# Loading the first quarter's mixed rows during the attention, and transposing the last samples' output behind three output tiles

## The chip, the cores and the metric

The kernel runs on one core of a Trainium2 chip. The core has five engines that run their own instruction queues and wait for each other on semaphores: TensorE (PE), VectorE (DVE), ScalarE (ACT), GpSimd (POOL) and SyncE (SP, which here only issues transfers). Sixteen DMA engines move data between the memory of the chip and the on-chip buffers; a transfer is issued from the queue of SP, ACT or POOL. The metric is the time of one execution on the device in microseconds (us); lower is better.

## The reference: what is computed

One layer of a decoder, for a prompt of 1024 tokens and for 8 samples of 8 new tokens each (together 1088 token columns), all in float32:

```python
h = rms_norm(x, norm1) * (1 + scale1) + shift1
z = h @ w_in                      # split into q, keys, values, gates, conv and pool inputs
o_attn = g[0] * o_cmp + g[1] * o_slc + g[2] * o_win     # three attention branches, gated
y_conv = conv_bg * short_conv(conv_cg * conv_h)
y_pool = multi_pool(pool_in)
x = x + gate1 * (concat[o_attn, y_conv, y_pool] @ w_out)
h = rms_norm(x, norm2) * (1 + scale2) + shift2
x = x + gate2 * (silu(h @ w_up_a) * (h @ w_up_b)) @ w_down
```

The compressed branch of the attention works on blocks of the keys and values that a small network (`compress`) makes; for the samples these come from a paged cache of 4096 positions each. The concatenation that goes into `w_out` is called the mixed rows here: 1024 channels (8 groups of 128) by 1088 columns.

## The kernel before

**Stages.** `build` runs three stages after one another. The first is the input projection, with the convolution and the pooling. The second is the attention: the prompt's (`prompt_attention`, 32 units of one block of 128 queries, one half of the heads and one branch, counted by `v_done`), the samples' (`sample_attention`, four pairs of samples with nine pieces each, counted by `u_done`) and beside them the compression of the samples' caches (`compress`, one batch per sample, counted by `cmp_done`). The third, `tail`, is the output projection, the norm, the up projection (in products of half matrices) and the down projection. A large product is made of three products of rounded parts: an operand is split by ACT into a high part (`split`, L175) and by DVE or POOL into the rest (L171), and `mm3` multiplies high by high, high by low and low by high.

**The mixed rows.** All three mixers write their part of the mixed rows to the buffer `mix_d` in the chip's memory: the convolution and the pooling in the first stage, the prompt's attention at L1205 after each second unit, and the samples' attention in `sample_combine` (L1406 on). The latter, once for each pair of samples `p`, makes on DVE a weighted sum of twelve partial results (`co`, L1428), transposes it on PE (`tr`, L143), copies it by DVE into `smo` (L1435) and stores it from SP's queue (L1439) into the columns from 1024 + 16 p.

**The output projection.** `output_projection` treats the 1088 columns as four quarters of 272. It goes through three groups: quarter 0, quarter 1, and quarters 2 and 3 together. In each group there are 8 output tiles `m` of 128 channels; a tile takes 24 matmuls of 272 columns for each quarter. `load` fetches a weight tile (`w_raw`, L1489, three buffers, SP's queue), `split` cuts it into `w_hi` and `w_lo` (two halves, nine buffers each). `fetch` (L1514) brings two channel groups of the mixed rows into `mixc` (four buffers), from SP's queue for quarter 0 and from ACT's for the others, and `mix` splits them into `mh` and `ml`. `x_load` (L1540) brings the rows of x from ACT's queue. The result of a tile goes by DVE (L1468) into x and from there to memory (`x_d`, L1559).

**What sets the order.** The program is a set of tasks (generators) with priorities; `run` picks the next one by an account of time that `use` keeps for each engine, and `yield` gives the account's time at which a task can go on. The framework below it then puts every engine's instructions in an order by its own simulated timeline. An engine works its queue strictly in that order. A buffer that is used again waits until what it held has been read. The pools of buffers lie on two stacks (left, right); a pool that is opened later takes the place of a closed one and waits for what lay there.

**What the change touches.** The buffers of `compress` and `compress_post` are `vt`, `pre`, `ksq`, `vcT` and `kvo` (L549 to L656), one of each. Their result is stored from POOL's queue (`cmp_d`, L669). The up projection keeps its hidden rows in `f_g` (L1662, four buffers).

Of the kernel before, what the change touches and what calls it, by code (L numbers as in the profile page):

```python
# [7 lines left out]
F32 = mybir.dt.float32  # L8
# [9 lines left out]
P = 128  # L18
D = 1024
KT = D // P  # L20
SEQ = 1024
NB = 8
NT = 8
# [3 lines left out]
HALF = 272  # L27
# [35 lines left out]
class Kernel:  # L63
# [476 lines left out]
    def compress(self, pool, batches, ahead):  # L540
        nc = self.nc
        last = batches[-1] * 4 + 3 + ahead
# [3 lines left out]
        for b in batches:  # L546
            yield from self.hold(lambda: self.post_free)
            self.post_free = False
            vt = pool.tile([P, 2, 256], F32, name="vt")  # L549
            pre = pool.tile([P, 2, 256], F32, name="pre")  # L550
            nc.vector.memset(pre[:, :, 255:256], 0.0)
            for half in range(2):
                uv = (yield from self.bank_of("S")).rearrange("p (v n) -> p v n", v=2)
                for q in range(2):
                    i = b * 4 + half * 2 + q
                    self.compress_load(i)
                    t, at = self.raw[i]
# [11 lines left out]
                r = self.compress_evac(uv, vt, pre, half)  # L569
# [22 lines left out]
    def compress_prompt(self, pool):  # L592
# [14 lines left out]
        self.post_free = False  # L607
        vt = pool.tile([P, 2, 256], F32, name="vt")
        pre = pool.tile([P, 2, 256], F32, name="pre")
        uv = (yield from self.bank_of("S")).rearrange("p (v n) -> p v n", v=2)  # L610
# [7 lines left out]
    def compress_post(self, pool, b, vt, pre, r, w=256):  # L618
# [16 lines left out]
        self.post_free = True  # L635
        sq = pool.tile([P, 256], F32, name="ksq")[:, 0:w]
        nc.scalar.activation(sq, o[0][:, 0:w], AF.Square)
        vc = pool.tile([P, 256], F32, name="vcT")[:, 0:w]
        nc.vector.tensor_copy(vc, o[1][:, 0:w])
# [9 lines left out]
        if b is None:  # L649
            self.tr(m[0:w, 256:256 + P], vc)  # L650
            nc.vector.tensor_copy(self.vcp, m[0:w, 256:256 + P])
            key, f = self.kcp, lambda a: a
        else:
            for h in range(2):
                self.tr(m[:, 256 + h * P:256 + (h + 1) * P], vc[:, h * P:(h + 1) * P])
            kv = pool.tile([P, 2, 256], F32, name="kvo")  # L656
            nc.vector.tensor_copy(kv[:, :, P:2 * P], m[:, 256:512].rearrange("p (h d) -> p h d", h=2))
            key, f = kv[:, :, 0:P], lambda a: a.rearrange("p (h c) -> p h c", h=2)
# [747 lines left out]
    def sample_combine(self, pool, st, p):  # L1406
# [16 lines left out]
        for x, (a, b) in enumerate(br):  # L1423
            nc.vector.tensor_scalar(w[:, a:b], w[:, a:b], ds_[:, 2 + x:3 + x], None, op0=OP.mult)
        o = pool.tile([P, P], F32, name="co", bufs=2)
        nc.vector.tensor_scalar(o, part[:, 11], gr[:, 0:1], None, op0=OP.mult)
        for c in range(11):
            nc.vector.scalar_tensor_tensor(o, part[:, c], w[:, c:c + 1], o, op0=OP.mult, op1=OP.add)  # L1428
        yield self.use("dve", 4.0, self.t["pe"]) + 0.5
        tr = yield from self.bank_of("S")  # L1430
        self.tr(tr[:, 0:P], o)
        mo = pool.tile([P, 4, 2, NT], F32, name="smo", bufs=2)
        for g in range(2):
# [3 lines left out]
                tr[s, 0:P].rearrange("p (b g r t) -> p g b r t", b=2, g=2, r=4)[:, g])  # L1437
        self.give("S", self.use("dve", 0.4, self.t["pe"]))
        nc.sync.dma_start(self.mix_d[:, 0:4, SEQ + 16 * p:SEQ + 16 * p + 16],  # L1439
                            mo.rearrange("p r b t -> p r (b t)"))  # L1440
        self.combined = p + 1

# [13 lines left out]
    def sample(self, opened, cp, batches):  # L1456
        share = lambda: 1.9 + 0.4 * (self.cmp_done - EARLY) / (NB - EARLY)
        self.spawn(share, self.compress(cp, batches, 0))
        sp = opened.enter_context(self.pool("samp", "left"))
        yield self.t["dve"]  # L1460
        self.spawn(lambda: 2 + 1.1 * self.u_done / 36, self.sample_attention(sp))


    def residual(self, out, acc, m, c0, n, gate, x, pool):
# [4 lines left out]
        if np_ < n:  # L1469
# [3 lines left out]
            nc.vector.tensor_tensor(r(out), r(x), tmp, op=OP.add)  # L1473
        return self.use("dve", 0.13 + np_ * 0.00104 + (0.27 if np_ < n else 0), self.t["pe"] + 0.1)

    def halves(self, a):
# [15 lines left out]
    def output_projection(self, wp, pool, nt, x1, opened):  # L1492
# [3 lines left out]
        todo = [m for _ in groups for m in range(KT)]  # L1496
        raw, ws, mx, parts = [], [], [], {}

# [8 lines left out]

        order = [(c, k) for c in range(4) for k in range(0, KT, 2)]

        def fetch():  # L1510
            if order:
                c, k = order.pop(0)
                t = pool.tile([P, 2, HALF], F32, name="mixc", bufs=4)
                (nc.sync if c == 0 else nc.scalar).dma_start(t, self.mix_d[:, k:k + 2, c * HALF:c * HALF + HALF])  # L1514
                mx.append((c, k, t, self.use("dma", 0.8, self.t["pe"]) + 2.2))
# [10 lines left out]

        fetch()
        load()
        for _ in range(3):
            fetch()  # L1530
        load()
# [12 lines left out]
        for cs in groups:  # L1544
            ss = {c: nt.tile([P, HALF], F32, name="n_ss", bufs=2) for c in cs}
            for m in range(KT):
                w = ws.pop(0)
                load()
                for c in cs:
                    yield max(w[0][2], parts[c, 0][2])  # L1550
                    acc = self.bank()
                    for k in range(KT):
                        wk = [self.halves(a)[:, k % 4] for a in w[k // 4][:2]]
                        self.mm3(acc[:, :HALF], wk, parts[c, k][:2], k == 0, k == KT - 1)
                    if c == cs[-1]:
# [103 lines left out]
    def up(self, fp, j, p, W, H, step):  # L1659
        nc = self.nc  # L1660
        bank = {}
        g = fp.tile([P, 2, HALF], F32, name="f_g", bufs=4)  # L1662
        t1 = lambda name: fp.tile([P, HALF], F32, name=name, bufs=1)
# [463 lines left out]
    def build(self):  # L2127
# [16 lines left out]
        self.tok_last = None  # L2144
        self.constants()
        st_ = self.pool("stream", "left")
        self.stream = st_.__enter__()
# [169 lines left out]
```

## Time and profile before

| | |
|---|---|
| median of 3 runs | 1677.42 us (1677.28 to 1678.26) |
| the profiled execution's own time | 1670.79 us |
| its span, first to last instruction | 1669.2 us |
| PE busy in the span | 1565.7 us, 94% |
| DVE, ACT, POOL busy | 1092.0, 777.8 and 660.9 us |
| mean granted TensorE clock | 0.975 |
| end of the attention's last matmul | 818.67 us |
| first matmul of the output projection | 834.46 us |

Times in the views are microseconds from the start of the span. A line of the timeline has the start, the duration, the engine, the line of the kernel with the operation, what is written and read, how many instructions are merged, and in brackets the idle time of the engine before it with what ended it. "SPq" and "ACTq" are the transfers that these queues issue. In a view of the waits a line says who waited for whom, in total us, how often, and the longest.

### The profile page before, as it was taken

The page shows a single profiled execution, that of the slowest core. Times are in us where ns is not written, and L with a number is a line of the kernel's source. Part 1 is how long each engine was busy: PE and PEld are TensorE (multiplying, and loading weights), DVE is VectorE, ACT ScalarE, POOL GpSimd, SP SyncE. Part 2 cuts the span into 40 slices and gives each one's busy share as a digit, 9 for nine tenths or more (in the row PEclk, how much of TensorE's full clock was granted, in tenths as well). Part 3 has the DMA queues.
Part 4 walks back from the last instruction along what each step waited for, and adds up shares of the span by engine and source line. Part 5 has one row for each costly group of instructions (what it writes and reads, how often), then busy time and mean ns, then how long its engine had stood idle before and what let it go on. Part 6 is the DMA issues. An engine that isn't in the chain of part 4 may idle for free. (4 is left out here: it accounts for less than half of the span.)

```text
span 1669.2 us, 35421 instructions
## 1 busy us (share of the span) xinstructions
PE 1565.7 (94%) x12569; PEld 1390.4 (83%) x12569; DVE 1092.0 (65%) x2633; ACT 777.8 (47%) x1829; POOL 660.9 (40%) x789
## 2 busy tenths in 40 slices
PE   6998999997999899899599989999999999899998
PEld 2898897896777666566399989999999999899988
DVE  4713233887555566766589878777777775577695
ACT  3522114335766667666467534433334433344463
POOL 3120110114333223223003366554555554778695
PEclk9999999998999899999899999999999999999999
DMA  9575765325457363344696564346443345966553
GB/s 342 196 261 160 204 174 167 126 101 156 127 178 214 110 193 97 91 127 139 197 323 194 197 215 175 141 145 231 146 143 141 137 145 198 397 232 241 187 168 122
DMA packets 195025, 302.10 MB, mean 181 GB/s; under 512 B 26353, under 2 KB 131378, under 8 KB 194530
## 3 DMA queue, kind: packets, MB, share of 16 engines
q1 hardware_dynamic: 174978, 272.20, 49.4%
q0 software_dynamic: 5856, 16.24, 3.2%
q10 hardware_dynamic: 14016, 11.41, 2.2%
q8 instruction: 100, 1.64, 0.4%
q14 instruction: 75, 0.61, 0.1%
HBM read 233.43 MB, written 70.53 MB: 182 GB/s over the span
## 5 line engine op out<-in xcount | busy, mean ns | idle before, releaser
L139 PE MATMUL bank<-b_hi,w_hi 128*128 128x272 f32 x1232 | 351.4, 290 | 6.0 <-DVE f_g L1677 2.9
L139 PE MATMUL bank<-b_lo,w_hi 128*128 128x272 f32 x1232 | 353.7, 289 | 2.5 <-DVE b_lo L171 2.5
L139 PE MATMUL bank<-b_hi,w_lo 128*128 128x272 f32 x1232 | 348.8, 288 | 0.9 <-DVE w_lo L171 0.9
L139 PEld LDWEIGHTS bank<-b_hi,w_hi 128*128 128x128 f32 x1232 | 230.6, 189 | 9.2 <-ACT b_hi L175 3.8
L139 PEld LDWEIGHTS bank<-b_lo,w_hi 128*128 128x128 f32 x1232 | 232.8, 189 | 3.4 <-DVE b_lo L171 3.3
L139 PEld LDWEIGHTS bank<-b_hi,w_lo 128*128 128x128 f32 x1232 | 230.8, 189 | 1.1 <-DVE w_lo L171 1.1
L1136 POOL TENSOR_SCALAR P<-P,st 128x128 f32<-128x128 f32 (+10 forms) x192 | 108.9, 581 | 229.6 <-DVE st L1132 130.9
L171 DVE TENSOR_TENSOR w_lo<-w_raw,w_hi 128x512 fp32r<-128x512 f32 (+2 forms) x121 | 117.0, 975 | 67.3 <-ACT w_hi L175 66.6
L139 PEld LDWEIGHTS bank<-stream 128*128 128x128 f32 x1056 | 131.1, 203 | 29.0 <-issue 14.6
L171 POOL TENSOR_TENSOR w_s<-w_raw 128x512 f32<-128x512 f32 (+1 forms) x88 | 125.8, 1429 | 67.8 <-DVE w_lo L171 55.2
L139 PE MATMUL bank<-stream 128*128 128x128 f32 x1056 | 138.4, 290 | 11.4 <-DMA wada<-in_wada 6.0
L171 POOL TENSOR_TENSOR x<-x,d_m 128x272 f32<-128x272 f32 x144 | 126.6, 901 | 34.4 <-DVE x L1879 19.6
L175 ACT ACTIVATE w_hi<-w_raw 128x512 fp32r<-128x512 f32 (+2 forms) x122 | 80.7, 677 | 125.9 <-PE bank L139 84.1
L1126 ACT ACTIVATE P<-P,st 128x128 f32<-128x128 f32 (+12 forms) x192 | 112.6, 588 | 44.5 <-DVE st L1120 28.5
L139 PE MATMUL bank<-h_hi,w_hi 128*128 128x384 f32 (+1 forms) x384 | 130.0, 338 | 0.5 <-DVE mod L1024 0.5
L139 PE MATMUL bank<-g,w_hi 128*128 128x272 f32 x616 | 121.6, 293 | 5.7 <-DVE x L1879 5.5
L139 PE MATMUL bank<-h_hi,w_lo 128*128 128x384 f32 (+1 forms) x384 | 126.4, 329 | 0.0
L171 DVE TENSOR_TENSOR w_lo<-w_s,w_hi 128x512 fp32r<-128x512 f32 (+1 forms) x124 | 116.3, 940 | 14.6 <-ACT w_hi L175 12.6
L139 PE MATMUL bank<-h_lo,w_hi 128*128 128x384 f32 (+1 forms) x384 | 125.7, 327 | 0.0
L139 PE MATMUL bank<-g,d_hi 128*128 128x272 f32 x616 | 120.3, 292 | 4.2 <-DVE x L1879 3.1
L1879 DVE SCALAR_TENSOR_TENSOR x<-bank,mod,x 128x272 f32<-128x272 f32 (+1 forms) x192 | 87.0, 476 | 38.3 <-PE bank L139 33.9
L139 PEld LDWEIGHTS bank<-g,w_hi 128*128 128x128 f32 x616 | 98.1, 191 | 7.3 <-DVE x L1879 6.1
(373 smaller groups left out, 3720.9 us busy)
## 6 DMA issues: line engine op xcount, KB each, us to landing
g_d<-f_s SPq DMA_DIRECT2D x57, 544.0 KB, 3.1
g<-g_d SPq DMA_DIRECT2D x56, 544.0 KB, 6.1
wada<-in_wada SPq DMA_DIRECT2D x96, 256.0 KB, 5.3
stream<-in_cacheA SPq DMA_DIRECT2D x192, 128.0 KB, 3.2
w_raw<-in_wup SPq DMA_DIRECT2D x40, 512.0 KB, 4.4
unit<-in_cacheB SPq DMA_DIRECT2D x152, 128.0 KB, 2.4
stream<-in_cacheB SPq DMA_DIRECT2D x104, 128.0 KB, 2.4
w_raw<-in_wout SPq DMA_DIRECT2D x24, 512.0 KB, 4.8
```

The costliest lines, as they stand in the source:

```text
L139: return self.nc.tensor.matmul(out, lhsT, rhs, start=start, stop=stop, skip_group_check=chain)
L171: (self.nc.vector if eng == "dve" else self.nc.gpsimd).tensor_tensor(out, a, b, op=op)
L175: self.nc.scalar.activation(hi, src, AF.Copy)
L1126: nc.scalar.activation(Ps, Ps, AF.Exp, scale=-1.0, bias=sy[:, g, 0:1], accum_out=sy[:, g, 1:2])
L1136: nc.gpsimd.tensor_scalar(Ps, Ps, sy[:, g, 3:4], 0.0, op0=OP.mult, op1=OP.add)
L1879: nc.vector.scalar_tensor_tensor(out[:, :n], acc[:, :n], self.mod[:, 5, m, 0:1], out[:, :n], op0=OP.mult, op1=OP.add)
```

## The change

The loads of quarter 0's mixed rows leave `output_projection` and become a task of the attention, `first_mix`, that waits until the eight batches of the compression are done and 14 units of the prompt's attention, and then issues the four loads from POOL's queue. The buffers for that come from a pool `base` that is opened at the beginning and never closed: four tiles of 128 x 2 x 272 (`pair`). The same four serve `compress` (in the place of `vt`, `pre`, `ksq` with `vcT`, and `kvo`), then the mixed rows of all quarters (in the place of `mixc`), and then the up projection (in the place of `f_g`). The columns of the first quarter belong to the prompt alone; of the samples' columns, 1024 to 1087, all lie in the last quarter. For the last pair of samples the transpose, the two copies and the store leave `sample_combine` (now `sample_store`) and stand behind the last matmul of output tile `m == 2` of quarter 0, with buffers of their own (`co3`, `smo3`).

```diff
@@ compress, compress_prompt, compress_post
-            vt = pool.tile([P, 2, 256], F32, name="vt")
-            pre = pool.tile([P, 2, 256], F32, name="pre")
+            vt = self.pair256()
+            pre = self.pair256()
...
-        sq = pool.tile([P, 256], F32, name="ksq")[:, 0:w]
+        both = self.pair256()
+        sq, vc = both[:, 0, 0:w], both[:, 1, 0:w]
...
-            kv = pool.tile([P, 2, 256], F32, name="kvo")
+            kv = self.pair256()
@@ sample_combine
-        o = pool.tile([P, P], F32, name="co", bufs=2)
+        o = pool.tile([P, P], F32, name="co", bufs=2) if p < 3 else self.co
...
-        yield self.use("dve", 4.0, self.t["pe"]) + 0.5
-        tr = yield from self.bank_of("S")
+        r = self.use("dve", 4.0, self.t["pe"]) + 0.5
+        if p < 3:
+            yield r
+            tr = yield from self.bank_of("S")
+            self.sample_store(p, tr, o, pool.tile([P, 4, 2, NT], F32, name="smo", bufs=2))
+            self.give("S", self.t["dve"])
+        self.combined = p + 1
+
+    def sample_store(self, p, tr, o, mo):
+        nc = self.nc
         self.tr(tr[:, 0:P], o)
...
@@ sample
+        self.spawn(1.95, self.first_mix())
+
+    def first_mix(self):
+        yield from self.hold(lambda: self.cmp_done == NB and self.v_done >= 14)
+        self.mix0 = []
+        for k in range(0, KT, 2):
+            t = self.pair()
+            self.nc.gpsimd.dma_start(t, self.mix_d[:, k:k + 2, 0:HALF])
+            self.mix0.append((0, k, t, self.use("dma", 0.8, self.t["pe"]) + 2.2))
...
+    def pair(self):
+        return self.base.tile([P, 2, HALF], F32, name="pair", bufs=4)
+
+    def pair256(self):
+        return self.pair().rearrange("p a b -> p (a b)")[:, 0:512].rearrange("p (a b) -> p a b", a=2)
@@ output_projection
-        raw, ws, mx, parts = [], [], [], {}
+        raw, ws, mx, parts = [], [], self.mix0, {}
...
-        order = [(c, k) for c in range(4) for k in range(0, KT, 2)]
+        order = [(c, k) for c in range(1, 4) for k in range(0, KT, 2)]
...
-                t = pool.tile([P, 2, HALF], F32, name="mixc", bufs=4)
-                (nc.sync if c == 0 else nc.scalar).dma_start(t, self.mix_d[:, k:k + 2, c * HALF:c * HALF + HALF])
+                t = self.pair()
+                nc.scalar.dma_start(t, self.mix_d[:, k:k + 2, c * HALF:c * HALF + HALF])
...
-        fetch()
         load()
-        for _ in range(3):
-            fetch()
         load()
         split()
         mix(4)
...
-                        self.mm3(acc[:, :HALF], wk, parts[c, k][:2], k == 0, k == KT - 1)
+                        last = self.mm3(acc[:, :HALF], wk, parts[c, k][:2], k == 0, k == KT - 1)
+                    if c == 0 and m == 2:
+                        with self.tc.issue_after(last.ins):
+                            self.sample_store(3, self.bank(), self.co, self.smo)
@@ up
-        g = fp.tile([P, 2, HALF], F32, name="f_g", bufs=4)
+        g = self.pair()
@@ build
+        self.base = self.ctx.enter_context(self.pool("base", "left"))
+        self.co = self.base.tile([P, P], F32, name="co3")
+        self.smo = self.base.tile([P, 4, 2, NT], F32, name="smo3")
```

Three places show how the instructions stand now. The first is ACT's queue where the attention ends and the output projection begins, before and after (`part` are the samples' partial results, `w_hi` and `mh` the high parts of the weights and of the mixed rows, `x1a` the rows of x of the first two quarters).

```order
L161 ACTIVATE part<-bank 128x128
L175 ACTIVATE w_hi<-w_raw 128x512 x7
L1540 DMA x1a_10498<-in_xT 128x2x272 x3
L175 ACTIVATE mh<-mixc 128x272 x2
L1540 DMA x1a_10498<-in_xT 128x2x272
L175 ACTIVATE mh<-mixc 128x272 x2
L1540 DMA x1a_10499<-in_xT 128x2x272
```

```order
L161 ACTIVATE part<-bank 128x128
L175 ACTIVATE w_hi<-w_raw 128x512 x6
L175 ACTIVATE mh<-pair 128x272 x8
L1558 DMA x1a_10495<-in_xT 128x2x272 x2
L1535 DMA pair<-mix_d 128x2x272 x3
L1558 DMA x1a_10495<-in_xT 128x2x272
L1535 DMA pair<-mix_d 128x2x272
L1558 DMA x1a_10495<-in_xT 128x2x272
L1558 DMA x1a_10496<-in_xT 128x2x272 x2
L175 ACTIVATE mh<-pair 128x272 x2
L175 ACTIVATE w_hi<-w_raw 128x512
```

Two more `w_hi` stand ahead of the last `part` in both. The eight `mh` of quarter 0 now stand together behind the eighth `w_hi`, and the ninth `w_hi`, the loads of x and those of quarter 1 follow them.

The second place is PE's queue at the same time (`spt` and `unit` belong to the samples' attention; `co` is transposed), before and after.

```order
L139 MATMUL bank<-unit,spt 64x128 x16
L143 MATMUL bank<-ident,co 128x128
L139 MATMUL bank<-mh,w_hi 128x272 x5
L139 MATMUL bank<-ml,w_hi 128x272
L139 MATMUL bank<-mh,w_lo 128x272
```

```order
L139 MATMUL bank<-unit,spt 64x128 x16
L139 MATMUL bank<-mh,w_hi 128x272 x3
L139 MATMUL bank<-ml,w_hi 128x272
L139 MATMUL bank<-mh,w_lo 128x272
```

The transpose of `co` is gone from there; it now stands between the third and the fourth output tile.

The third place is POOL's queue, where the compression's last batch is stored (`P` are the prompt's attention weights), and where the output projection begins (`b_t` belongs to the up projection's operands). Before and after:

```order
L1136 TENSOR_SCALAR P<-P,st 128x512 x8
L669 DMA cmp_d<-kvo 128x512
L1136 TENSOR_SCALAR P<-P,st 128x39 x2
L1136 TENSOR_SCALAR P<-P,st 128x640 x2
...
L1136 TENSOR_SCALAR P<-P,st 128x640 x2
L171 TENSOR_TENSOR w_lo<-w_raw,w_hi 128x512
L171 TENSOR_TENSOR b_t<-x1a_10498 128x272
```

```order
L1136 TENSOR_SCALAR P<-P,st 128x512 x8
L1475 DMA pair<-mix_d 128x2x272 x2
L669 DMA cmp_d<-pair 128x512
L1475 DMA pair<-mix_d 128x2x272
L1136 TENSOR_SCALAR P<-P,st 128x39 x2
L1475 DMA pair<-mix_d 128x2x272
L1136 TENSOR_SCALAR P<-P,st 128x640 x2
...
L1136 TENSOR_SCALAR P<-P,st 128x640 x2
L171 TENSOR_TENSOR w_lo<-w_raw,w_hi 128x512 x2
L171 TENSOR_TENSOR b_t<-x1a_10495 128x272
```

Two loads stand ahead of the last store of the compression, one behind it, and one behind two of the weights' instructions. At the beginning of the output projection POOL has one subtraction of the weights more, the one of the eighth half (`w_lo`), which DVE did before.

More of the change, by code (lines that the diff above doesn't have):

```diff
@@ L607, in compress_prompt @@
         self.post_free = False
-        vt = pool.tile([P, 2, 256], F32, name="vt")
-        pre = pool.tile([P, 2, 256], F32, name="pre")
+        vt = self.pair256()
+        pre = self.pair256()
         uv = (yield from self.bank_of("S")).rearrange("p (v n) -> p v n", v=2)
@@ L635, in compress_post @@
         self.post_free = True
-        sq = pool.tile([P, 256], F32, name="ksq")[:, 0:w]
+        both = self.pair256()
+        sq, vc = both[:, 0, 0:w], both[:, 1, 0:w]
         nc.scalar.activation(sq, o[0][:, 0:w], AF.Square)
-        vc = pool.tile([P, 256], F32, name="vcT")[:, 0:w]
         nc.vector.tensor_copy(vc, o[1][:, 0:w])
@@ L1428, in sample_combine @@
             nc.vector.scalar_tensor_tensor(o, part[:, c], w[:, c:c + 1], o, op0=OP.mult, op1=OP.add)
-        yield self.use("dve", 4.0, self.t["pe"]) + 0.5
-        tr = yield from self.bank_of("S")
+        r = self.use("dve", 4.0, self.t["pe"]) + 0.5
[7 more added lines that the diff above has]
+        nc = self.nc
         self.tr(tr[:, 0:P], o)
-        mo = pool.tile([P, 4, 2, NT], F32, name="smo", bufs=2)
         for g in range(2):
@@ L1437, in sample_combine @@
                 tr[s, 0:P].rearrange("p (b g r t) -> p g b r t", b=2, g=2, r=4)[:, g])
-        self.give("S", self.use("dve", 0.4, self.t["pe"]))
+        self.use("dve", 0.4, self.t["pe"])
         nc.sync.dma_start(self.mix_d[:, 0:4, SEQ + 16 * p:SEQ + 16 * p + 16],
                             mo.rearrange("p r b t -> p r (b t)"))
-        self.combined = p + 1
     def attention(self, ap, kp_, opened):
```

## The prediction

> **What bounds the kernel now.** The page comes first: the span, how busy the engines are, and then the stretches around the place of the change.
>
> ```profile
> span 1669.2 us, 35421 instructions
> PE 1565.7 (94%) x12569; PEld 1390.4 (83%) x12569; DVE 1092.0 (65%) x2633; ACT 777.8 (47%) x1829; POOL 660.9 (40%) x789
> ```
>
> ```profile
> core 0: us, PE busy (x) PEld busy (x) DVE busy (x) ACT busy (x) POOL busy (x), PEclk, DMA share, GB/s
> 810.00:820.00 10.00, 8.02 (x96) 5.91 (x92) 6.89 (x24) 6.14 (x18) 0.00 (x0) 1.00 0.63 217
> 820.00:830.00 10.00, 0.47 (x1) 0.18 (x1) 6.45 (x15) 3.24 (x6) 0.00 (x0) 0.69 0.73 230
> 830.00:840.00 10.00, 5.54 (x33) 5.54 (x34) 3.13 (x8) 3.00 (x8) 0.00 (x0) 0.62 1.01 318
> 840.00:850.00 10.00, 10.00 (x82) 10.00 (x81) 6.96 (x15) 5.74 (x13) 0.00 (x0) 1.00 1.10 369
> 850.00:870.00 20.00, 20.00 (x160) 19.92 (x159) 17.63 (x35) 14.78 (x33) 1.28 (x1) 1.00 1.01 337
> ```
>
> PE is busy for 94% of the span, so time is won only where it stands still. One such place lies between 818 and 835 us, where the attention hands over to the output projection. The timeline of PE shows the gap in two parts:
>
> ```profile
> 816.70 1.97 PE L139 MATMUL bank<-unit,spt 128*64 128x128 f32 x32 [0.65 <-DVE cs L1422]
> 825.54 0.47 PE L143 MATMUL bank<-ident,co 128*128 128x128 f32 x1 [6.87 <-DVE co L1428]
> 834.46 1.50 PE L139 MATMUL bank<-mh,w_hi 128*128 128x272 f32 x5 [8.45 <-ACT mh L175]
> 835.76 0.43 PE L139 MATMUL bank<-ml,w_hi 128*128 128x272 f32 x1
> 835.98 0.43 PE L139 MATMUL bank<-mh,w_lo 128*128 128x272 f32 x1
> 837.55 0.29 PE L139 MATMUL bank<-mh,w_hi 128*128 128x272 f32 x1
> 837.68 0.29 PE L139 MATMUL bank<-ml,w_hi 128*128 128x272 f32 x1
> ```
>
> First 6.87 us for the weighted sum `co`, then 8.45 us for the first `mh`. What ends the second wait is a chain through four queues, read from their timelines:
>
> ```profile
> 825.14 0.34 DVE L1428 SCALAR_TENSOR_TENSOR co<-part,cw,co 128x128 f32<-128x128 f32 x1
> 827.82 0.45 DVE L1435 COPY smo<-bank 64x64 f32<-64x64 f32 x2
> 828.30 0.38 SPq L1439 DMA_DIRECT2D mix_d<-smo  x1
> 828.73 2.84 SPq L1514 DMA_DIRECT2D mixc<-mix_d  x4
> 823.87 1.15 ACT L175 ACTIVATE w_hi<-w_raw 128x512 fp32r<-128x512 f32 x2 [2.40 <-DMA w_raw<-in_wout]
> 826.55 0.63 ACT L175 ACTIVATE w_hi<-w_raw 128x512 fp32r<-128x512 f32 x1 [1.53 <-DMA w_raw<-in_wout]
> 833.97 0.43 ACT L175 ACTIVATE mh<-mixc 128x272 fp32r<-128x272 f32 x1 [6.79 <-DMA mixc<-mix_d]
> ```
>
> The copies wait for PE's transpose and stand behind weights on DVE; SP stores them at 828.30 and only then issues the loads of quarter 0, though these columns were complete long before; they land about 5 us later, and PE starts 0.49 us after ACT does. From there on PE hardly waits:
>
> ```profile
> 834.40:930.00 95.60, 94.14 (x732) 93.51 (x733) 86.93 (x180) 62.54 (x146) 23.86 (x23) 0.98 0.77 249
> PE bank L139 <- ACT mh L175: 8.4, 1, 8.4
> PE bank L139 <- DVE n_ss L171: 1.1, 1, 1.1
> PE bank L139 <- DVE w_lo L171: 0.9, 1, 0.9
> PE bank L139 <- ACT w_hi L175: 0.3, 1, 0.3
> ```
>
> Until 960 us it waits 2.3 us for other things. So what the start gains, PE keeps, as long as weights and rows come as early too.
>
> **The change part by part.** *The start (gain 9.0 us).* The chain through `co`, the copies, the store and the loads no longer leads to the first `mh`. What now stands ahead of it on ACT are the eight `w_hi`, of which the last two wait for the fourth weight tile and end at 823.87 + 1.15 = 825.02. That tile's load has the same predecessors on SP and DVE as before. The first `mh` then starts at about 825.0 in place of 833.97, and with the same 0.49 us PE starts at about 825.45 in place of 834.46: 9.0 us. PE then still stands still for 6.8 us, so the bound from above for this term is 15.3 us (both gaps), reached only if ACT split the rows ahead of the weights, which the new order excludes. The eight `mh` follow each other faster than PE asks for them: ACT needs 0.43 us or less for one, PE three matmuls of 0.22 us at its first pace.
>
> *The slow first matmuls (0).* From 834.46 to 837.5 the matmuls follow each other at 0.22 us (835.76, 835.98), afterwards at 0.13 us (837.55, 837.68): a cold start of 3.0 us that costs some 13 x 0.1 = 1.3 us. The transpose at 825.54 was slow as well, behind a gap of 6.87 us:
>
> ```profile
> L143 PE MATMUL bank<-ident,co x4: 327/328/472, 589.8 to 825.5; 128*128 128x128 f32 x4
> ```
>
> The new gap is as long, so the cold start is paid in both. The Trainium skill (TensorE: Matmul & The Clock Gate, Part 1) says that the clock rises only after one busy window of about 3.4 us, by windows that run freely. The trace's 3.0 us agrees; but if a stall fell into that window, by the rule another one could pass, which at these paces is 3.4 x 0.44 = 1.5 us (an estimate from that page); the sum below would be 6.4 in place of 7.9.
>
> *POOL's subtraction (loss 0.8 us).* The eighth `w_lo` moves from DVE to POOL, where it takes 1.28 us from about 825.1. The trace has one such meeting:
>
> ```profile
> 865.19 1.28 POOL L171 TENSOR_TENSOR w_lo<-w_raw,w_hi 128x512 fp32r<-128x512 f32 x1 [65.07 <-ACT w_hi L175]
> 865.32 2.30 DVE L171 TENSOR_TENSOR w_lo<-w_raw,w_hi 128x512 fp32r<-128x512 f32 x2
> 857.15 1.28 DVE L171 TENSOR_TENSOR w_lo<-w_raw,w_hi 128x512 fp32r<-128x512 f32 x2
> ```
>
> Two subtractions on DVE took 2.30 us beside it and 1.28 us without: one stood still until POOL was done. The first `ml` would so begin at 825.1 + 1.3 = 826.4 and end at 826.8; PE, with three matmuls ahead of it (825.45 + 0.68 = 826.1), waits about 0.8 us. Bounds: 0 if they miss each other, 1.3 if all of it falls on PE. I take 0.8.
>
> *The transpose on PE (loss 0.3 us).* It moves out of a gap into a stretch where PE is full: between 0.33 us (the median above) and nothing if it overlaps its neighbours. I take 0.3. The two copies (0.45 us) go to DVE, which is busy for 86.93 of 95.60 us there, and wait for nobody's matmul, since the last quarter is read much later; without that cover they cost 0.45. The store goes into SP's queue behind the third tile's rows; behind it stand weight tiles that are three buffers ahead.
>
> *Other bubbles (0, from -1.1 to 3).* The ninth `w_hi` stands behind the `mh` of quarter 1, whose loads start only at about 829. By the order, the fifth tile's second half is split at about 837.5, and PE asks for it at 825.45 + 1.3 + 13.5 = 840.2; the margin is 2 to 3 us. If it fails, that much again is lost; if the `n_ss` wait of 1.1 us goes, that is won.
>
> *The loads on POOL (0).* Four transfers, at 0.59 us on the queue each by the store next to them:
>
> ```profile
> 585.69 0.59 POOL L669 DMA_DIRECT2D cmp_d<-kvo  x1 [4.67 <-DVE co L1428]
> 588.89 0.62 POOL L1136 TENSOR_SCALAR P<-P,st 128x39 f32<-128x39 f32 x2 [2.62 <-DVE st L1132]
> 593.72 2.15 POOL L1136 TENSOR_SCALAR P<-P,st 128x640 f32<-128x640 f32 x4 [4.21 <-DVE st L1132]
> DMA to landing us min/median/max: 3.6/3.6/3.6
> ```
>
> Two fit into the 4.67 us ahead of the store. The fourth takes the buffer that this store reads, so it waits for its landing, 585.69 + 3.6 = 589.3, then 0.6 us; behind it stands `P` at 593.72, whose readers are PE's transposes. 3 us are left. At the longest landing of these stores (9.1 us in the last case below) it would be 1.7 us late. The rows then have 230 us to arrive.
>
> Sum: 9.0 - 0.8 - 0.3 = 7.9 us. The profiled execution took 1670.79 us (span 1669.2 and 1.6 around it), so its like would take 1662.9. The median of the runs lies 6.63 us above it, 1677.42: I predict **1669.5 us**.
>
> **The rivals.** *The transfers set the pace: gain 3.2 to 5.9.* From 830 to 870 the DMA engines are at 1.0. If what they carry, not PE, decides when tiles five to eight are ready, only what they are spared counts: 4 x 272 KB, 1.1 MB, at 337 to 369 GB/s 3.2 us, and at most the idle 27% of 820 to 830, 2.7 us. That is 1671.5 to 1674.2. For it: the full rows. Against: PE is full in the same rows, and among those transfers are the rows of x for quarters 2 and 3, needed 48 us later.
>
> *The gain is given back at the up projection: 1677.4.* There DVE splits operands while PE waits. If DVE's backlog set its end, PE would only wait longer. Against: DVE has caught up with PE just ahead of it and waits for it:
>
> ```profile
> 935.24 0.43 DVE L1468 SCALAR_TENSOR_TENSOR x1b<-bank,mod,x1b 128x208 f32<-128x208 f32 x1 [0.35 <-PE bank L139]
> ```
>
> and over 834 to 930 it has 8.7 us to spare.
>
> *The four shared buffers hold up the compression: slower.* A batch's first buffer can now be one whose store has to land first; two of ACT's first copies carry such a wait in the new order. If each meets a store just issued, it costs up to the longest landing, 2 x 9.1 = 18.2 us, less 7.9: 1687.7. It decides from 7.9 us that PE really waits.
>
> ```profile
> 512.62 0.54 POOL L669 DMA_DIRECT2D cmp_d<-kvo  x1 [4.81 <-DVE kvo L664]
> 544.19 0.27 ACT L583 ACTIVATE vt<-bank 64x128 f32<-64x128 f32 x1 [2.34 <-PE bank L139]
> 550.34 0.54 POOL L669 DMA_DIRECT2D cmp_d<-kvo  x1 [4.69 <-DVE kvo L664]
> DMA to landing us min/median/max: 2.3/2.8/9.1
> ```
>
> Against: the last batch's copy at 544.19 stands ahead of the store at 550.34, so it can only wait for the one at 512.62, landed long before.
>
> **How the numbers follow.** Forecast (1667 to 1671.5) 0.67; transfers 0.15; given back, or no change worth the name, 0.12; slower 0.06. The range: from 1666.5 (9.0 and the 1.1 us of `n_ss`, and half a microsecond of scatter) up to 1675.0, which takes in the transfers' case. A measurement can tell 0.2%, 3.35 us, from no change: faster is below 1674.1. That holds for the forecast and for nearly all of the transfers' case: 0.80; within 0.2% 0.14; slower 0.06.
>
> **What would show it.** PE's timeline: no transpose of `co` in the gap, one gap of about 6.8 us ended by ACT's `mh`, first matmul of the projection 9.0 us earlier relative to the end of the attention (16 us before, 7 then). A slow first `ml` beside POOL's `w_lo`. The waits of PE behind it: about 2 to 3 us until the up projection; far more by `w_hi` or `w_lo` would mean the transfers' case. The loads from POOL near 585, with `P` not later. If the attention ends later than 818.7, or PE's waits in the up projection grow by several us, I am wrong.

## The result

The changed kernel is slower: 1685.44 us (median of 9 executions, 1682.69 to 1691.49) against 1677.42 us (9 executions, 1673.39 to 1679.12) of the kernel before beside it. The ratio is 1.0055, 95% interval 1.0040 to 1.0071, so 0.4 to 0.7% slower. I had forecast 1669.5, faster by 0.5%.

The profiled execution took 1686.37 us. The page and the timeline of PE after the change:

```profile
span 1684.8 us, 35425 instructions
PE 1579.6 (94%) x12569; PEld 1398.4 (83%) x12569; DVE 1094.4 (65%) x2632; ACT 778.4 (46%) x1829; POOL 666.0 (40%) x794
```

```profile
822.96 1.97 PE L139 MATMUL bank<-unit,spt 128*64 128x128 f32 x32 [0.65 <-DVE cs L1422]
831.60 1.05 PE L139 MATMUL bank<-mh,w_hi 128*128 128x272 f32 x3 [6.67 <-ACT mh L175]
833.02 0.60 PE L139 MATMUL bank<-ml,w_hi 128*128 128x272 f32 x1 [0.37 <-DVE ml L171]
...
836.59 0.38 PE L139 MATMUL bank<-ml,w_hi 128*128 128x272 f32 x1
836.80 0.29 PE L139 MATMUL bank<-mh,w_lo 128*128 128x272 f32 x1
```

The handover is as forecast. The transpose is gone from it, one gap of 6.67 us is left, and the first projection matmul comes 6.7 us after the end of the attention's last matmul (822.96 + 1.97 = 824.93) instead of 15.8. The time is lost elsewhere. From the first and last matmuls of each kind, the span falls into these pieces (us):

| | before | after | difference |
|---|---|---|---|
| end of the attention's last matmul | 818.7 | 824.9 | +6.3 |
| from there to the first `mh,w_hi` | 15.8 | 6.7 | -9.1 |
| first to last `mh,w_hi` (projection) | 100.2 | 111.6 | +11.4 |
| to the first `g,w_hi` (up projection) | 477.7 | 478.9 | +1.2 |
| to the first `g,d_hi` (start of the down projection) | 26.3 | 32.8 | +6.5 |
| to the last `g,d_hi` | 225.0 | 224.5 | -0.5 |

The 9.1 us are won and 18 are lost in two places. The first row can't be put down to the change: in two more profiles of the kernel before, the attention's last matmul ends at 820.4 and 824.3 us.

**The projection.** The waits of PE between 815 and 950 us, and the windows (PE, PEld, DVE, ACT, POOL busy, granted clock, share of the DMA engines, GB/s):

```profile
PE bank L139 <- ACT mh L175: 6.8, 2, 6.7
PE bank L139 <- ACT w_hi L175: 3.0, 4, 1.5
PE bank L139 <- DVE w_lo L171: 2.5, 3, 1.2
PE bank L139 <- DVE ml L171: 1.7, 3, 1.0
```

```profile
831.00:851.00 20.00, 19.03 (x133) 18.71 (x134) 13.31 (x30) 10.11 (x26) 1.06 (x1) 0.86 1.05 353
851.00:861.00 10.00, 8.75 (x67) 8.22 (x66) 5.55 (x12) 4.45 (x10) 0.00 (x0) 1.00 1.02 339
861.00:871.00 10.00, 8.27 (x61) 7.45 (x60) 9.38 (x18) 8.15 (x17) 1.62 (x1) 1.00 0.93 312
871.00:881.00 10.00, 7.47 (x54) 6.67 (x53) 10.00 (x24) 9.09 (x21) 0.86 (x1) 1.00 0.51 152
```

Before, PE got through 80 to 82 matmuls in every 10 us from 840 to 870 us. Now there are 67, 61 and 54. In 851 to 861 DVE and ACT stand still half the time as well. So there neither is too slow; each waits for another. (From 861 on DVE is nearly full, but so it is in a version below in which PE is full beside it.) An output tile of one quarter is 24 matmuls and takes 3.0 us where nothing is missing. The time of each such group, from its first matmul to that of the next group (so a wait for the next group's weights counts in the group before), with "lead" for how long before the group's first matmul the second half of its `w_hi` was ready:

```
group (quarter, m)  (0,4) (0,5) (0,6) (0,7) (1,0) (1,1) (1,2) (1,3) (1,4) (1,5)
before: took us      3.00  3.00  3.00  3.00  3.00  3.26  3.20  3.00  3.00  3.68
before: lead us       6.0   5.7   4.9   1.7   2.5   1.5   2.1   3.8   2.5   1.5
after:  took us      3.00  3.00  4.21  3.59  4.79  3.59  3.96  4.73  4.62  3.01
after:  lead us       4.6   3.0   4.0  -0.5   0.0  -0.5   0.3   2.9  -0.5   1.6
```

From tile (0,7) on the weights come just as PE asks for them or too late. The groups (0,6) to (1,4) lose 8.5 us over 3.0 each, before 0.5. The rest of the 11.4 us lies mostly in the first group (5.83 us for 4.47) and where quarter 3 is first used (6.89 for 4.60). ACT's timeline shows why the weights are late at (0,7), whose weight tile SP requested at 845.61:

```profile
845.61 0.33 SPq L1510 DMA_DIRECT2D w_raw<-in_wout  x1
847.97 0.62 ACT L175 ACTIVATE w_hi<-w_raw 128x512 fp32r<-128x512 f32 x1
851.73 0.55 ACTq L1558 DMA_DIRECT2D x1b<-in_xT  x1
852.32 0.43 ACT L410 ACTIVATE n_t<-x1a 128x272 f32<-128x272 f32 x1 [1.68 <-DMA pair<-mix_d]
852.82 1.22 ACTq L1558 DMA_DIRECT2D x1b<-in_xT  x2
854.08 0.43 ACT L410 ACTIVATE n_t<-x1a 128x272 f32<-128x272 f32 x1 [1.33 <-DVE x1a L1483]
855.40 0.57 ACTq L1558 DMA_DIRECT2D x1b<-in_xT  x1
856.07 1.15 ACT L175 ACTIVATE w_hi<-w_raw 128x512 fp32r<-128x512 f32 x2 [1.55 <-PE bank L139]
```

The tile lands 5.8 us after its request, at 851.4; its `w_hi` is made at 856.07, 4.7 us later. In that time ACT's queue works off four loads of `x1b`, the rows of x for the last two quarters, which nobody reads for another 40 us. ACT computes nothing until each of them is issued: the two `n_t` start 0.04 us behind the end of an issue (851.73 + 0.55 = 852.28, 852.82 + 1.22 = 854.04) and `w_hi` 0.10 us behind the last (855.97). The idle times of 1.68, 1.33 and 1.55 us that the view puts down to a transfer, to DVE and to PE end with these issues. The Trainium skill (TensorE: Matmul & The Clock Gate, Part 1) says that ACT's queue is strictly first in, first out. The trace agrees: nothing overtook the loads.

The same tile before the change:

```profile
843.58 0.34 SPq L1489 DMA_DIRECT2D w_raw<-in_wout  x1
850.18 0.55 ACTq L1540 DMA_DIRECT2D x1b<-in_xT  x1
854.12 1.14 ACT L175 ACTIVATE w_hi<-w_raw 128x512 fp32r<-128x512 f32 x2
```

It landed 6.1 us after its request, at 849.6, and its conversion began 4.5 us later. So ACT's queue held it about as long, at no cost: PE, which had begun the projection 2.9 us later by the span's time, asked for it at 856.93. After the change the request comes 2.0 us later and PE would have asked at 855.54, had the weights been there. The hold is old; the earlier start lays it bare.

**The down projection.** A part of an output accumulator is cleared by a memset on DVE, and PE waits for what DVE does behind it. The timeline after the change, with a store from POOL's queue:

```profile
1436.22 0.73 POOL L1755 DMA_DIRECT2D g_r<-f_T  x1 [0.30 <-POOL f_T L171]
1442.62 0.48 DVE L2019 MEMSET x<- 128x512 f32 x1 [14.95 <-DMA g<-g_d]
```

PE's only wait from 1410 to 1490 us in the same kernel:

```profile
PE bank L139 <- DVE x L1900: 11.3, 1, 11.3
```

The same two of the kernel before, from the timeline and from the waits between 1400 and 1470 us:

```profile
1426.33 0.48 DVE L1998 MEMSET x<- 128x512 f32 x1 [8.44 <-POOL f_T L171]
```

```profile
PE bank L139 <- DVE x L1879: 4.8, 1, 4.8
```

PE waits 6.5 us longer. Ahead of the memset in DVE's queue stand three instructions that only wait:

```profile
L2019 DVEq EVENT_SEMAPHORE  x3: 21/50/50, 1442.2 to 1442.4; - x3
```

The first of them waits for the store issued at 1436.22, which lands 6.0 us later, at 1442.2. Then the others pass at once, so this store is the releaser, though the view names a load. In a second profile of the changed kernel it is the same store (landed 1438.97, the first wait over at 1439.02). Before, the memset was released when POOL had read `f_g` for the last time (1426.2). The accumulators of the down projection lie where the up projection's buffers lay. The stores whose semaphores the memset waits for are of `f_g` before the change and of `f_T` after it. I infer from these waits, not from addresses, that what is cleared lay on `f_g` and, since `f_g` has left that pool, now lies on `f_T`, which is written and stored last.

### The profile page after: what moved, and what is told of

It reads as the page before. It is cut to its first block, busy times and chain, and to the rows that moved or that the text cites. A ratio compares the mean times of both kernels' runs of the same rounds, so it can differ in the third digit from the quotient of the medians.

```text
span 1684.8 us, 35425 instructions
## 1 busy us (share of the span) xinstructions
PE 1579.6 (94%) x12569; PEld 1398.4 (83%) x12569; DVE 1094.4 (65%) x2632; ACT 778.4 (46%) x1829; POOL 666.0 (40%) x794
## 5 line engine op out<-in xcount | busy, mean ns | idle before, releaser
L171 DVE TENSOR_TENSOR w_lo<-w_s,w_hi 128x512 fp32r<-128x512 f32 (+1 forms) x124 | 115.9, 938 | 13.6 <-ACT w_hi L175 11.4
L1900 DVE SCALAR_TENSOR_TENSOR x<-bank,mod,x 128x272 f32<-128x272 f32 (+1 forms) x192 | 86.8, 475 | 36.3 <-PE bank L139 33.1
```

Source lines behind the costliest of these rows:

```text
L171: (self.nc.vector if eng == "dve" else self.nc.gpsimd).tensor_tensor(out, a, b, op=op)
L1900: nc.vector.scalar_tensor_tensor(out[:, :n], acc[:, :n], self.mod[:, 5, m, 0:1], out[:, :n], op0=OP.mult, op1=OP.add)
```

## The experiments

The table has every run; "start", "projection" and "down" are the second, third and fifth row of the table above. Ratios are to the kernel before, run on the same chip in the same study (medians from 1676.0 to 1677.75); they are worked out from the single executions and differ by up to 0.2% from the quotient of the medians. The changed kernel was not run in the studies of the first seven rows, and its own time is known only as 1685.44 (ratio 1.0055) and, again, 1680.81 (1.0033); so what a version gains against it is read from the stages of the profiles first. The expectations count the projection as 112.0 and 100.6 us where the table above has 111.6 and 100.2.

| run | time us | ratio (95%) | start | projection | down |
|---|---|---|---|---|---|
| accumulators in another order | 1677.24 | 0.9985 (0.9965 to 1.0006) | 6.8 | 109.6 | 26.0 |
| x's loads behind `w_hi` | 1678.80 | 0.9984 (0.9965 to 1.0004) | 6.7 | 101.6 | 32.8 |
| transpose put back | 1680.53 | 1.0015 (0.9993 to 1.0038) | 9.8 | 104.3 | 33.1 |
| x's loads on POOL | 1684.20 | 1.0040 (1.0021 to 1.0059) | 6.8 | 109.7 | 33.6 |
| both repairs | 1669.79 | 0.9968 (0.9950 to 0.9986) | 6.7 | 102.5 | 26.2 |
| shared ring alone | 1678.41 | 1.0013 (0.9994 to 1.0032) | 9.7 | 104.0 | 33.3 |
| both repairs, rows split first | 1674.51 | 1.0000 (0.9982 to 1.0018) | 3.2 | 108.6 | 27.2 |
| ring alone, both repairs | 1669.25 | 0.9965 (0.9948 to 0.9981) | 9.8 | 99.4 | 27.1 |
| both repairs, transpose put back | 1668.62 | 0.9968 (0.9951 to 0.9985) | 9.7 | 99.5 | 27.1 |
| changed kernel again | 1680.81 | 1.0033 (1.0013 to 1.0052) | 6.8 | 110.1 | 34.1 |
| kernel before again | 1675.43 | 1.0003 (0.9981 to 1.0024) | 15.6 | 100.2 | 27.9 |
| kernel before, third profile | 1679.11 | 1.0009 (0.9988 to 1.0030) | 15.4 | 101.4 | 27.3 |

### Accumulators in another order

```diff
-        for c in (3, 2, 0, 1):
+        for c in (2, 3, 0, 1):
             x2[c] = dp.tile([P, KT, HALF], F32, name=f"x2{c}")
```

> The changed kernel with one line of the down stage altered: the four output accumulators are allocated in the order chunk 2, 3, 0, 1 instead of 3, 2, 0, 1; nothing is left out. Theory A (an accident of addresses): in the changed kernel the memset of accumulator chunk 3 waits 15.0 us, because its memory now lies where the last f_T tile was, whose store was issued at 1436.22 and landed about 1442.2 us; TensorE waits 11.3 us for it, 4.8 us in the kernel before. With the order turned round, the memset follows at about the distance of before, TensorE's longest wait there is 4.8 to 5.5 us and the time falls by 6 to 6.5 us, to about 1679. Rival (the down stage is late because its weights and g tiles are late, the memset only shows it): the wait stays near 11 us under another releaser and the time stays at 1685.

Measured: 1677.24 us. The memset in its timeline, and PE's wait there:

```profile
1421.47 0.48 DVE L2019 MEMSET x<- 128x512 f32 x1
```

```profile
PE bank L139 <- DVE x L1900: 4.7, 1, 4.7
```

The memset waits for nothing, PE 4.7 us where it waited 4.8 before the change. The time is 8.2 us below the first study's 1685.44 and 3.6 below the 1680.81 of the second time; the 6.5 us of the wait lie between. One line that only changes addresses removes the wait: theory A holds. The projection, untouched, loses as before (109.6).

### x's loads behind the conversions

```diff
-        self.nc.scalar.activation(hi, src, AF.Copy)
+        self.last_hi = self.nc.scalar.activation(hi, src, AF.Copy)
@@ x_load
-                nc.scalar.dma_start(dst, src)
+                with self.tc.issue_after(self.last_hi.ins):
+                    nc.scalar.dma_start(dst, src)
```

> The changed kernel, where each load of the residual input x1 on ScalarE's queue is put behind the newest w_hi conversion that stands ahead of it in the program, instead of where the scheduler floats it; nothing is left out. Theory B (ScalarE is held by issuing loads that wait for earlier transfers, and the weight conversions behind them are late): the projection's 32 groups of 24 matmuls, 112.0 us in the changed kernel and 100.6 before, take 102 to 106 us, the groups (0,6) to (1,4) lose under 4 us of the 8.5 us above 3.0 each that they lose now, and the time falls by 5 to 9 us. Rival C (bytes: all 16 DMA engines are busy from 831 to 871 us and the weights are late whatever the order): the projection stays at 110 to 112 us. Rival D (the stock of converted weights is small because TensorE starts 9 us sooner after the attention, whatever queues the loads stand in): 107 to 112 us.

Measured: 1678.80 us, projection 101.6. ACT's timeline at tile (0,7), then the windows, then PE's longest waits from 822 to 935 us:

```profile
848.32 1.15 ACT L175 ACTIVATE w_hi<-w_raw 128x512 fp32r<-128x512 f32 x2 [1.44 <-DMA w_raw<-in_wout]
849.02 1.93 ACTq L1559 DMA_DIRECT2D x1b<-in_xT  x2
```

```profile
851.00:861.00 10.00, 10.00 (x82) 10.00 (x82) 8.82 (x20) 7.88 (x19) 0.00 (x0) 1.00 1.01 354
861.00:871.00 10.00, 9.88 (x77) 9.61 (x77) 8.72 (x16) 6.86 (x14) 1.41 (x1) 1.00 1.05 382
871.00:881.00 10.00, 10.00 (x82) 10.00 (x81) 10.00 (x24) 9.34 (x22) 0.77 (x1) 1.00 0.75 225
```

```profile
PE bank L139 <- ACT mh L175: 6.7, 1, 6.7
PE bank L139 <- DVE n_ss L171: 1.3, 1, 1.3
```

The conversion of tile (0,7) now waits for its own load alone and starts 7.75 us earlier (848.32 against 856.07): the load is requested 3.2 us earlier, at 842.41, and the rest is the hold in ACT's queue, which is gone. The loads of x follow. The leads of (0,6) to (1,4) are 4.1 to 6.9 us; these groups lose 0.9 us. The DMA engines are as full as in the changed kernel (1.01 and 1.05 against 1.02 and 0.93), and PE is full beside them: the bytes did not set the pace, their order did. Rivals C and D fall, and theory B holds in size (its 102 to 106 us are 101.6 here, about 102 as the expectation counts). PE starts as early as in the changed kernel, so the early start alone does not cost the time; it costs it together with this order.

### The transpose put back

The condition `if p < 3` goes out of the combination of the samples, so that all four pairs are transposed and stored there, and the piece behind `m == 2` goes out of the projection.

> The changed kernel with the transpose of the last samples put back to the end of the attention, while the first quarter's mixed rows are still loaded during the attention; nothing is left out. Theory D (what is gained at the start of the projection is stock that its weights lose): the first projection matmul comes 1 to 4 us later after the attention's last PV matmul than in the changed kernel, the projection is shorter by about as much, and the time is the same within 3 us. Rival E (the moved transpose itself disturbs the projection: its store stands in SyncE's queue ahead of a weight load, 853.64 against 851.8 us): the start is later by 1 to 4 us, but the projection takes 103 to 106 us, and the time falls by 4 to 7 us.

Measured: 1680.53 us. The start is 3.2 us later and the projection 7.4 us shorter: by the numbers E. But the scheduler orders other loads differently here too (the first load of `x1b` is issued at 836.86, in the changed kernel at 841.33), so that this run doesn't show that the store in SP's queue was the cause; the last runs below show what the transpose is worth without the other loss.

### x's loads from POOL

```diff
-                nc.scalar.dma_start(dst, src)
+                nc.gpsimd.dma_start(dst, src)
```

> The changed kernel with the 16 loads of the residual input x1 issued by GpSimd (idle from 833 to 861 us) instead of ScalarE; same bytes; nothing is left out. Theory B (ScalarE held by issuing): the projection takes 102 to 106 us instead of 112.0, and the time falls by 5 to 9 us. Rival C (bytes): no change in the projection, 110 to 112 us. Rival D (stock): 107 to 112 us. If the loads issued earlier by an idle GpSimd crowd the weight loads, it is longer than 112 us.

Measured: 1684.20 us, projection 109.7. POOL's and ACT's timeline:

```profile
833.86 1.53 POOL L1558 DMA_DIRECT2D x1b<-in_xT  x2
836.67 0.75 ACT L175 ACTIVATE mh<-pair 128x272 fp32r<-128x272 f32 x2 [6.33 <-DMA pair<-mix_d]
841.49 0.76 ACT L175 ACTIVATE mh<-pair 128x272 fp32r<-128x272 f32 x2 [4.06 <-DMA pair<-mix_d]
842.14 0.61 ACT L175 ACTIVATE w_hi<-w_raw 128x512 fp32r<-128x512 f32 x1
```

B's expectation missed. ACT issues no x any more, but it now waits for the rows of quarter 1, whose transfers run beside those of x, and `w_hi` stands behind these rows in its queue. So it is not the issuing on ACT alone. In both versions that lose, loads needed late go out ahead of what is needed soon, whichever queue they are in. How much of the 10 us belongs to ACT's held queue and how much to the crowded transfers isn't separated: putting x's loads behind the conversions changed both.

### Both repairs

The two edits above together.

> The changed kernel with both edits that took time off it one at a time: the accumulators allocated in the order 2, 3, 0, 1 and the residual loads held behind the newest w_hi conversion; nothing is left out. Theory A plus B (two separate losses, 6.5 us in the down stage and 10 us in the projection): the projection takes 102 us, the distance from the first g matmul to the first d_hi matmul 26 us, and the time is 1669 to 1673 us, faster than both kernels. Rival (one loss hides the other, since a stage that starts sooner waits longer for the same transfers): 1676 to 1679 us.

Measured: 1669.79 us; projection 102.5, down 26.2. Both losses are gone at once, and this version beats both kernels (0.9968 to the kernel before).

### The shared ring alone

The spawn of the early loads is taken out, quarter 0 is fetched again in the projection, and the transpose is put back.

> One part of the change alone: the compression and the feed-forward gates share the ring of four pair buffers, as in the changed kernel, but the first quarter's rows are loaded at the start of the projection and the last samples are transposed at the end of the attention, as before. Nothing is left out. Theory F (the shared buffers slow the attention: from the first to the last attention matmul it took 434.8 to 438.1 us in five profiles of kernels that share, 431.3 us in the one profile of before): 435 to 438 us of attention here too, the projection 100 to 102 us, the down stage 6 us late because the f_g ring is gone from its old place, and a time of 1683 to 1688 us. Rival G (the attention differs from run to run, or by the early loads): 431 to 434 us of attention and a time of 1681 to 1684.

Measured: 1678.41 us. The attention takes 432.1 us, as G has it. My description was wrong in one point: with buffers that are free so early the scheduler moved SP's four loads to 565.6 to 615.7 us, so this is again a kernel with early loads, from another queue. That is why the start is 9.7 and not 15.6 us, and the time is below what both expected. The down projection is late (33.3) as expected, with neither early loads from POOL nor a moved transpose: that loss belongs to the ring. The projection takes 104.0 us in place of the 100 to 102 that I expected; with x's loads behind the conversions it takes 99.4 (below).

### The kernel before again

> The kernel before once more, for a second profile of it. Theory F (shared buffers cost the attention 4 to 6 us): the attention takes 430 to 432.5 us again. Rival G (it varies between executions): 433 to 437 us.

Measured: 432.6 us of attention, between the two; a third profile was taken below.

### Rows split first

On top of both repairs:

```diff
         load()
-        load()
-        split()
         mix(4)
+        load()
+        split()
```

> The version with both edits, in which the first quarter's rows are also split into mh and ml ahead of the second and third weight blocks' conversions, where ScalarE otherwise converts eight w_hi first and waits 2.4 us for a weight load; nothing is left out. If the 6.7 us that TensorE waits for mh after the attention is ScalarE's order: that wait falls to 2 to 4 us, and the time by 2 to 4 us below that of the version with both edits. If the weights' lead (5 us ahead of their use there) is what the projection needs: the wait falls, the projection grows by as much, and the time is that of both edits within 1 us.

Measured: 1674.51 us, 4.7 more than without this edit. PE's timeline:

```profile
823.46 0.65 PE L139 MATMUL bank<-mh,w_hi 128*128 128x272 f32 x3 [3.17 <-ACT mh L175]
827.15 0.59 PE L139 MATMUL bank<-ml,w_hi 128*128 128x272 f32 x1 [3.05 <-DVE ml L171]
```

PE starts 3.5 us sooner after the attention, and the projection grows by 6.1. The second expectation has the direction and not the size. PE stops again after three matmuls, 3.05 us for `ml`, and at the groups (1,4) and (1,5), which took 6.9 and 5.1 us, the latter with its weights 0.5 us late. PE was started before what it needs had a lead.

### Ring alone and early loads alone, with both repairs

> The shared ring alone (transpose at the end of the attention, the first quarter's rows loaded from SyncE's queue, which the scheduler moved to 565.6 to 615.7 us once their buffers were free that early) with both repairs: accumulator order 2, 3, 0, 1, and the residual loads behind the newest w_hi conversion. Nothing is left out. The shared ring alone had 9.7 us from the last PV matmul to the first projection matmul, a projection of 104.6 us and 33.3 us from the first g to the first d_hi matmul, at 1678.4. If the repairs add up here too: 9.7, 101 to 103 and 26 to 27 us, and a time of 1667 to 1671, the same as the changed kernel with both repairs (1669.8) within 2 us, so that the moved transpose is worth at most what the later start costs. If the moved transpose is worth its 3 us of start once the weights are in time: 1671 to 1674.

> The changed kernel with both repairs and the transpose put back to the end of the attention; the first quarter's rows are still loaded by GpSimd during the attention. Nothing is left out. Against the version with both repairs (1669.8): the start is 3 us later (9.8 instead of 6.7 us after the last PV matmul), the projection 101 to 103 us as there. If the moved transpose is worth its 3 us: 1672 to 1674. If the later start is made up in the projection: 1669 to 1671.

Measured: 1669.25 and 1668.62 us. Start and projection together are 109.2 us in both, with the transpose at the end of the attention, and 109.2 with the transpose moved. PE's timeline with it put back:

```profile
830.20 0.47 PE L143 MATMUL bank<-ident,co 128*128 128x128 f32 x1 [6.93 <-DVE co L1428]
832.99 1.47 PE L139 MATMUL bank<-mh,w_hi 128*128 128x272 f32 x5 [2.32 <-DVE smo L1442]
```

The wait for `mh` is gone here too (2.32 us in place of 8.45 behind the transpose). So the early loads make the gain at the start, and the moved transpose is worth nothing that can be measured: its 3 us of start are lost again in the projection. That they come off the lead of the weights is likely, not shown. Nor was the kernel before run with x's loads behind the conversions; its 116.0 us of start and projection against 109.2 differ mostly at the start (15.8 against 9.7).

### The attention, two more profiles

> The changed kernel once more, for a second profile. Six profiles of kernels with GpSimd's early loads show 432.4 to 438.2 us from the first attention matmul to the end of the last PV matmul, three profiles without them 431.3 to 432.6. Theory H (the early loads cost the attention some 4 us, by 10 us more of halved TensorE clock): 434 to 439 us. Rival (the spread is between executions): 430 to 434 us is as likely. Projection 110 to 112 us, first g to first d_hi matmul 32 to 33 us in either case.

> The kernel before once more, for a third profile. Theory H (the attention is 4 us shorter without GpSimd's early loads): 430 to 433.5 us of attention, 34 us or less of halved clock in it. Rival (spread between executions): 434 us or more. Projection 100 to 101 us, first g to first d_hi matmul 26 to 28 us.

From the first to the last matmul of the attention the kernel before took 431.3, 432.6 and 437.8 us, the changed kernel 437.4 and 437.8. Windows of the attention in the first and the third profile of the kernel before:

```profile
387.40:818.70 431.30, 397.96 (x3999) 281.75 (x3999) 272.82 (x1193) 273.83 (x754) 130.59 (x231) 0.96 0.50 148
386.50:824.30 437.80, 404.21 (x4000) 286.93 (x3999) 272.73 (x1193) 274.35 (x754) 132.34 (x233) 0.95 0.49 146
```

The same kernel differs by 6.5 us with itself: theory H's forecast for the kernel before missed, and the +6.3 us in the first table lies within this spread. A smaller effect isn't excluded: nine profiles with early loads from POOL average 435.9 us (432.4 to 438.2), five without 433.7 (431.3 to 437.8). The changed kernel's second profile repeats the two losses (110.1 and 34.1). Over three profiles of before and two of after the start has changed by 6.7 - 15.6 = -8.9, the projection by 110.9 - 100.6 = +10.3 and the down projection by 33.4 - 27.2 = +6.2: together 7.6 us. The medians differ by 8.0 us in the first study and by 4.8 in the last (1680.81 against 1676.0).

## Why the prediction was wrong

- **The start of the projection, 9.0 us:** right (9.1), with the wait that was named: one gap of 6.67 us, ended by ACT's `mh` behind eight `w_hi`.
- **The slow first matmuls, 0:** too low by about 1 us. Matmuls run at the slow pace from 831.60 to 836.8, 5.2 us instead of 3.0. At 0.227 against 0.125 us apart, 2.2 us more of it cost 2.2 x 0.45 = 1.0. The granted clock was 0.50 from 829.95 to 836.78, so PE began 1.65 us after the clock had fallen; before, it was 0.50 from 823.85 to 837.50, and PE began 3.0 us ahead of its end. The Trainium skill (TensorE: Matmul & The Clock Gate, Part 1) has windows of about 3.4 us that run freely, and the trace agrees: the two stretches are 6.83 and 13.65 us, two and four times 3.41. But the stall that the prediction named as what would let another window pass isn't shown to be the cause. There was one (0.37 us at 833.02), yet with both repairs and the transpose put back, where none stands there, the slow stretch was 5.8 us long.
- **POOL's subtraction, 0.8:** it happened where it was forecast, at half the size, as the 0.37 us wait for `ml`. The transpose, 0.3: the group that begins behind it took 3.09 us for 2.99 before. The loads on POOL, 0: right. They took 0.70 to 0.77 us of its queue each in place of 0.59, and `P` waited for DVE, not for them.
- **"Other bubbles (0, from -1.1 to 3)":** this is the first term that failed. I checked one tile, the fifth, and its margin was there (4.6 us). The weights run out three tiles later. Before, PE stood still for 15 us while the weights' pipeline filled; starting 9 us sooner takes that lead away (15.2 us at the first tile, now 6.1), and from (0,7) on PE pays for loads of x that stand ahead of a conversion on ACT. It cost 10 us, not 0 to 3. Turning that one order round gave 8 to 10 us back (101.6 against 109.6 to 111.6).
- **The down projection has no term in my sum.** That is the second step that failed. I followed the four shared buffers where they are used and not what moves into the space they leave. Taking `f_g` out of its pool made the accumulators' memset wait for the last store of `f_T`: 6.5 us, shown by turning round the accumulators' order and by the ring alone, which has the loss too.
- **The rivals.** "The transfers set the pace" named the right place with the wrong mechanism: full DMA engines, but with the same bytes in another order PE is full beside them. By the prediction's own sign, more waits for `w_hi` and `w_lo` (5.5 us), it would have been taken for true. "Given back at the up projection" didn't happen (477.7 and 478.9). "The shared buffers hold up the compression" didn't either: the ring alone had 432.1 us of attention. The slower side came from a mechanism that none of them named.
- **The range.** By its own terms (9.0, 1.1 and 0.5 us) the low end comes to 1666.8, not 1666.5.
- **Profile and median.** I carried the 6.6 us between the profiled execution and the median along as an offset, which was sound; but two single profiles can't be compared stage by stage below some 6 us in the attention. An attention that ends later than 818.7 was named as a sign of being wrong; it is none, since the kernel before itself ended it at 824.3.

## What to carry to other kernels

Idle time ahead of a pipeline also fills that pipeline: before counting an earlier start as gained, follow the lead of the operands (request, landing, conversion, first use) through all tiles until it stops shrinking, and put loads that are needed late behind conversions that are needed soon. When a buffer changes its pool, look at what later pools now lie on, and at what releases that memory last. Take a second and a third profile of the kernel before, since a stage of one kernel can differ by several us between executions: its attention took 431.3 to 437.8 us, its up projection 477.7 to 482.0.

## What the runs showed of the hardware

The attention of one and the same kernel took 431.3 to 437.8 us. DVE and ACT were busy for the same time in both executions (272.8 and 272.7, 273.8 and 274.4 us), but PE was 6.25 us longer busy with the same 4000 matmuls (397.96 and 404.21): the granted clock was halved for 34.1 us of it in one and for 47.8 us in the other. Half of the extra 13.7 us is 6.8 us, about the whole difference. In all fourteen profiles the clock was halved 4.8 to 5.4 us after the attention's last matmul, and around the handover it stayed so for 6.8, 10.2 or 13.7 us. The memory accident has a number as well: a store issued beside a stream of loads took 6.0 us to land, and one memset that waited for it cost PE 6.5 us.
